# A recurrent layer whose odd chunks swap partition halves between the two heads of a pair

## The chip, the cores and the metric

The kernel runs on one core of a Trainium2 chip. Five engines work side by side on that core: TensorE (PE in the profile, with its weight loads as PEld), VectorE (DVE), ScalarE (ACT), GpSimd (POOL) and SyncE (SP), which here issues most DMAs. The metric is the device time of one execution in microseconds (us). The kernel before took 1336.81 us, the median of three runs between 1336.61 and 1337.48 us. A difference below about 0.2% can't be told from no change.

TensorE's array has 128 rows and 128 columns. The rows that a matmul uses are the partitions of its two operands, the columns are the partitions of its result in PSUM. A product with 64 rows and 64 columns therefore uses one quarter of the array, called a quadrant here and written (row half to column half): (0 to 0), (0 to 64), (64 to 0), (64 to 64).

## The reference

The reference is a two-layer encoder trunk on 512 frames of width 1024. Layer 0 mixes time by an RWKV-7 recurrence with 12 heads of 64 and attends to 256 memory tokens, layer 1 mixes by attention over chunks, and each is followed by a convolutional gated feed-forward part. The change concerns only the recurrence of layer 0, whose state is updated frame by frame:

```python
def step(state, inp):
    r_t, w_t, k_t, v_t, a_t, b_t = inp
    sa = jnp.einsum('bhvk,bhk->bhv', state, a_t)
    state = (state * w_t[:, :, None, :] + sa[..., None] * b_t[:, :, None, :]
             + v_t[..., None] * k_t[:, :, None, :])
    return state, jnp.einsum('bhvk,bhk->bhv', state, r_t)
```

Around it, projections give r, k, v, a and the decay w, and the result y is normalised per head, gets a bonus term and is multiplied by a gate.

## The kernel before

The 512 frames are cut into 8 chunks of 64, and the 12 heads into 6 pairs. A pair fills the 128 partitions: head 0 lies on partitions 0 to 63 (`HS[0]`), head 1 on 64 to 127 (`HS[1]`). The recurrence is computed in its chunked form. Within a chunk everything becomes products of 64 by 64 blocks, the coupling of the frames inside a chunk is a triangular system whose inverse is built from blocks of 16 and 32, and only the state is handed from chunk to chunk.

Three Python generators issue the work of a pair. `prepare` does the three dense projections (24 weight tiles, three matmuls of 128x512 each), the keys and decays `KB`, `AR`, `E`, and the inversion of the 16-blocks on DVE with four small DMA round trips. `front` multiplies `KB` by `AR` into the masked table `ML` (line 879, evicted by DVE at 882), turns `AR` and `v` into rows in `VT` (`rows_av`, lines 903 and 905, evicted by ACT at 907), turns `KB` into rows (893, evicted at 896), and joins the inverse blocks to 32 in `Tt`. `back` does the rest:

- transposes the inverse blocks on DVE (984), and multiplies a 32-block of `ML` by them (989), evicted by ACT into `X5` (993);
- multiplies `ML` by the value rows (997), evicted into slot 2 of `VT` (998);
- completes the inverse to 64 (1003, evicted at 1007);
- applies the inverse to slots of `VT` (1013), evicted into `W` (1014) and back into `VT` (1016);
- multiplies `W` by `ML` (1024), evicted by DVE into `MQ` (1025, 1026);
- forms the chunk's contribution to the state `G` (1032, 1033) and the output inside the chunk (1041), runs the chain over chunks (1046, 1047, 1051), normalises and gates.

Each fp32 matmul of the program appears as two instructions in the trace, so the 16 products (8 chunks, 2 heads) of a step count as 32. The results of 997 and 989 for all eight chunks lie in one PSUM bank. Steps 1013 and 1024 are done in two halves of four chunks, one bank and one `yield` each. In all these steps the two heads of one chunk alternate, and both head's products use the same two quadrants for every chunk: (0 to 0) and (64 to 64) in 1013 and 1024, (64 to 0) and (0 to 64) in 997. Only `rows_av` visits all four: head h goes (h to h) for `AR` and (h to 1-h) for `v`.

The order of the work is set by `weave`. It holds, for each generator, the sum of the costs that it has yielded, divided by an expected total, and lets the one go on that is furthest behind; a second number in a `yield` keeps a generator away for that many planner nanoseconds. Weave number st runs `back` of pair st-1, `front` of pair st and `prepare` of pair st+1 together, so the dense matmuls of `prepare` fill the time in which the small products wait for evictions. A last weave runs `back` of pair 4, `front` and `back` of pair 5, the memory attention, and part of the output projection. The framework's scheduler may still move an instruction past another that it holds not ready. Each engine then works strictly through its own list.

Small products go to a PSUM pool "S" of four banks, shared by `front`, `back`, `prepare` and the memory attention. `psy` and `psc` have a pool of two, dense projections another two. A bank is given out again when its eviction is done.

Of the kernel before, what the change touches and what calls it, by code (L numbers as in the profile page):

```python
# [18 lines left out]
P = 128  # L19
# [93 lines left out]
def trunk_kernel(ctx, tc, A, out):  # L113
# [40 lines left out]
    def ups():  # L154
        return ps_s((P, 8, 64))
# [547 lines left out]
    U = [(c, h, HS[h], HS[1 - h]) for c in range(NCH) for h in range(2)]  # L703
    MC = 16 * 80

    d2s = [dp.tile([2, 8, 2, 4, NCH, 32], F32, name="d2" + "ab"[n_], tag="d2" + "ab"[n_]) for n_ in range(2)]

    def prepare(i, T):
# [160 lines left out]
    def front(i, T, nxt=None):  # L869
# [4 lines left out]
        for c4 in range(2):  # L874
            ps = [ps_s((P, 4, 128)) for _ in range(2)]
            for c in range(4):
                cc = c4 * 4 + c
                for h in range(2):
                    PE.matmul(ps[h][:, c], KB[HS[h], cc, 1 - h:3 - h].rearrange("p s t -> p (s t)"),
                              AR[HS[h], cc].rearrange("p s t -> p (s t)"), start=True, stop=True)  # L880
            for h in range(2):
                V.tensor_tensor(ML[:, h, c4 * 4:c4 * 4 + 4, 0:128], ps[h][:],
                                C("m1").unsqueeze(1).to_broadcast([P, 4, 128]), op=ALU.mult)
            yield 1000
# [4 lines left out]
        def rows_kb():  # L889
            ps = [ups(), ups()]  # L890
            for c in range(8):
                for h in range(2):
                    PE.transpose(ps[h][:, c], KB[HS[h], c, 1 - h:3 - h].rearrange("p s t -> p (s t)"),
                                 cst[HS[h], I64:I64 + 64])
            for h in range(2):
                SC.copy(ML[:, h, :, 128:192], ps[h][:])


        def rows_av():
            ps = [ups(), ups()]  # L900
            for c in range(8):
                for h in range(2):
                    PE.matmul(ps[h][HS[h], c], AR[HS[h], c, 0], cst[HS[h], I64:I64 + 64], start=True, stop=True)
                for h in range(2):
                    PE.matmul(ps[h][HS[1 - h], c], v[HS[h], c], C("blkc", h * 64, 64)[HS[h]], start=True, stop=True)
            for h in range(2):
                SC.copy(VT[:, h], ps[h][:])

        rows_av()
        yield 1000  # L910
# [68 lines left out]
    def back(i, T, dst, tiles=own_tiles, go=None):  # L979
        Rq, dE, bon, ML, VT, Tt = (T[n] for n in ("Rq", "dE", "bon", "ML", "VT", "Tt"))  # L980
        W, MQ, X5, Tl, g2h, g2l, bank = tiles()

        for lo in (slice(0, 32), slice(64, 96)):
            V.transpose(Tl[lo], Tt[lo, :, 0:32])

        ps = ups()
        for c, h, ap, vp in U:
            lo, hi_ = slice(h * 64, h * 64 + 32), slice(h * 64 + 32, h * 64 + 64)
            PE.matmul(ps[hi_, c, 0:32], ML[lo, h, c, 32:64], Tl[lo, c], start=True, stop=True,
                      tile_position=(h * 64, h * 64 + 32))  # L990
        for h in range(2):
            hi_ = slice(h * 64 + 32, h * 64 + 64)
            SC.copy(X5[hi_], ps[hi_, :, 0:32])
        yield 650
        ps = ups()
        for c, h, ap, vp in U:
            PE.matmul(ps[ap, c], ML[vp, h, c, 0:64], VT[vp, h, c], start=True, stop=True)
        SC.copy(VT[:, 2], ps[:])
        yield MC
        ps = ups()  # L1000
        for c, h, ap, vp in U:
            lo, hi_ = slice(h * 64, h * 64 + 32), slice(h * 64 + 32, h * 64 + 64)
# [3 lines left out]
            lo = slice(h * 64, h * 64 + 32)  # L1006
            SC.copy(Tt[lo, :, 32:64], ps[lo, :, 0:32])
        yield 650, 400
        for c4 in (slice(0, 4), slice(4, 8)):
            ps = ps_s((P, 4, 2, 64))  # L1010
            for c in range(c4.start, c4.stop):
                for h in range(2):
                    PE.matmul(ps[HS[h], c % 4], Tt[HS[h], c], VT[HS[h], h:3:2 - h, c], start=True, stop=True)
            SC.copy(W[:, c4], ps[:, :, 0])
            for h in range(2):
                SC.copy(VT[HS[h], h, c4], ps[HS[h], :, 1])
            yield 1100
        G, St = VT[:, 2], W
        yield 0, 300
        for c4 in (slice(0, 4), slice(4, 8)):  # L1020
            ps = ps_s((P, 4, 128))
            for c in range(c4.start, c4.stop):
                for h in range(2):
                    PE.matmul(ps[HS[h], c % 4], W[HS[h], c], ML[HS[h], h, c, 64:192], start=True, stop=True)
            V.tensor_tensor(MQ[:, c4, 64:128], ps[:, :, 64:128], C("i64").unsqueeze(1).to_broadcast([P, 4, 64]), op=ALU.add)
            V.tensor_tensor(MQ[:, c4, 0:64], ps[:, :, 0:64], Rq[:, c4], op=ALU.add)
            yield 1100
        g2 = tmp(F32, (P, P))
        nc.sync.dma_start(g2, A["g2"][i])
        psg = ups()  # L1030
        for c, h, ap, vp in U:
            PE.matmul(psg[ap, c], ML[:, h, c, 128:192], VT[:, h, c], start=True, stop=True)
# [5 lines left out]
        psy = bank((P, 8, 64))  # L1038
        for c in range(8):
            for h in range(2):  # L1040
                PE.matmul(psy[HS[h], c], VT[:, h, c], ML[:, h, c, 64:128], start=c == 0, stop=False)
        yield 1700
        for c in range(8):
            if 0 < c < 7:
# [27 lines left out]
        dst(i, yc, pg)  # L1072
        yield 1080

    BACK_COST = 2 * 650 + 2 * MC + 4 * 1100 + 1700 + 6 * 150 + 7 * 150 + 700 + 1080

    mixd = dp.tile([4, P, S], F32, name="mixd", tag="mixd")

# [455 lines left out]
```

## Time and profile before

| Quantity | Value |
| --- | --- |
| Median of three runs | 1336.81 us (1336.61 to 1337.48) |
| Span of the profiled execution, first to last instruction | 1335.7 us |
| What lies around the span, median less span | 1.1 us |
| PE busy over the span | 1308.9 us (98%) |
| DVE and ACT busy | 926.4 us and 683.5 us |
| Stretch with the six weaves | about 88 to 345 us |
| Mean granted TensorE clock | 0.995 |

In the profile a line number is that of the kernel before. A group or timeline row names the engine, the line, the operation, the tile written and the tiles read, the part of the array (rows*columns), the moving operand's shape, and the count. Timeline rows begin with the start and the length. A matmul's length contains its passage through the array, so the pace of a series is read from the start of the series to the start of what follows, divided by the count. In square brackets stands idle time before an instruction, and what ended it.

### The profile page before, as it was taken

The page shows a single profiled execution, that of the slowest core. Times are in us where ns is not written, and L with a number is a line of the kernel's source. Part 1 is how long each engine was busy: PE and PEld are TensorE (multiplying, and loading weights), DVE is VectorE, ACT ScalarE, POOL GpSimd, SP SyncE. Part 2 cuts the span into 40 slices and gives each one's busy share as a digit, 9 for nine tenths or more (in the row PEclk, how much of TensorE's full clock was granted, in tenths as well). Part 3 has the DMA queues.
Part 4 walks back from the last instruction along what each step waited for, and adds up shares of the span by engine and source line. Part 5 has one row for each costly group of instructions (what it writes and reads, how often), then busy time and mean ns, then how long its engine had stood idle before and what let it go on. Part 6 is the DMA issues. An engine that isn't in the chain of part 4 may idle for free. (4 is left out here: it accounts for less than half of the span.)

```text
span 1335.7 us, 24426 instructions
## 1 busy us (share of the span) xinstructions
PE 1308.9 (98%) x9838; PEld 1099.3 (82%) x9838; DVE 926.4 (69%) x1822; ACT 683.5 (51%) x1166; POOL 20.1 (2%) x45
## 2 busy tenths in 40 slices
PE   9999999999999999999999999999999999999996
PEld 7787777777788899998888877786888999988885
DVE  7966766766669898887343675657689988893224
ACT  6666656665445445464232576657454444562221
POOL 0000000000000000000000000000000000000000
PEclk9999999999999999999999999999999999999998
DMA  5365344351232434223333323241324423223322
GB/s 197 110 187 109 88 96 96 86 115 55 96 105 84 142 95 127 71 64 98 94 107 104 120 87 96 88 130 51 111 87 134 124 67 111 80 76 103 100 87 78
DMA packets 65730, 135.42 MB, mean 101 GB/s; under 512 B 19792, under 2 KB 25296, under 8 KB 65616
## 3 DMA queue, kind: packets, MB, share of 16 engines
q1 hardware_dynamic: 63168, 124.94, 30.7%
q0 software_dynamic: 2448, 8.91, 3.8%
q8 instruction: 77, 1.26, 0.4%
q14 instruction: 37, 0.30, 0.1%
HBM read 127.53 MB, written 6.29 MB: 100 GB/s over the span
## 5 line engine op out<-in xcount | busy, mean ns | idle before, releaser
L176 DVE TENSOR_TENSOR wlo<-wraw,whi 128x1024 fp32r<-128x1024 f32 (+1 forms) x139 | 165.4, 1190 | 143.0 <-PE psd L208 131.3
L170 ACT CAST whi<-wraw 128x1024 fp32r<-128x1024 f32 (+1 forms) x156 | 159.9, 1026 | 167.3 <-DMA wraw<-in_ffn_out_dram 51.7
L204 PE MATMUL psd<-r1h,whi 128*128 128x512 f32 (+1 forms) x383 | 152.3, 399 | 0.1
L205 PE MATMUL psd<-r1l,whi 128*128 128x512 f32 x320 | 126.0, 394 | 0.0
L170 ACT CAST whi<-raw 128x1024 fp32r<-128x1024 f32 x88 | 82.9, 943 | 76.0 <-PE psf L420 41.8
L176 DVE TENSOR_TENSOR wlo<-raw,whi 128x1024 fp32r<-128x1024 f32 x88 | 95.6, 1086 | 15.2 <-ACT whi L170 15.2
L208 PE MATMUL psd<-r1h,wlo 128*128 128x512 f32 (+1 forms) x383 | 104.2, 397 | 0.0
L204 PEld LDWEIGHTS psd<-r1h,whi 128*128 128x128 f32 x383 | 72.0, 188 | 16.7 <-issue 2.7
L208 PEld LDWEIGHTS psd<-r1h,wlo 128*128 128x128 f32 x383 | 68.6, 188 | 14.7 <-issue 1.4
L420 PE MATMUL psf<-r2h,whi 128*128 128x256 f32 x308 | 77.3, 283 | 0.5 <-ACT tmp L442 0.5
L420 PE MATMUL psf<-r2l,whi 128*128 128x256 f32 x308 | 77.2, 283 | 0.0
L204 PE MATMUL psd<-r2h,whi 128*128 128x512 f32 (+1 forms) x184 | 71.1, 390 | 0.1
L205 PE MATMUL psd<-r2l,whi 128*128 128x512 f32 (+1 forms) x184 | 69.9, 383 | 0.0
L238 ACT ACTIVATE tmp<-xT 128x512 f32<-128x512 f32 x27 | 17.0, 631 | 103.0 <-DVE xT L497 88.3
L205 PEld LDWEIGHTS psd<-r1l,whi 128*128 128x128 f32 x320 | 60.2, 188 | 10.9 <-issue 0.2
L420 PEld LDWEIGHTS psf<-r2h,whi 128*128 128x128 f32 x308 | 59.1, 192 | 0.9 <-ACT tmp L442 0.7
L420 PEld LDWEIGHTS psf<-r2l,whi 128*128 128x128 f32 x308 | 59.1, 192 | 0.2
L422 PE MATMUL psf<-r2h,wlo 128*128 128x256 f32 x308 | 49.5, 283 | 0.0
L208 PE MATMUL psd<-r2h,wlo 128*128 128x512 f32 (+1 forms) x184 | 47.1, 386 | 0.0
L393 ACT ACTIVATE tmp<-tmp 128x512 f32<-128x512 f32 x44 | 27.7, 630 | 33.6 <-DVE tmp L392 33.1
L420 PE MATMUL psf<-r1h,whi 128*128 128x256 f32 x176 | 44.2, 284 | 0.3 <-ACT tmp L442 0.3
L204 PE MATMUL psd<-hl,whi 128*128 128x512 f32 (+1 forms) x119 | 44.4, 377 | 0.0
(468 smaller groups left out, 3326.7 us busy)
## 6 DMA issues: line engine op xcount, KB each, us to landing
wraw<-in_ffn_in_dram SPq DMA_DIRECT2D x44, 512.0 KB, 3.6
raw<-in_ffn_in_dram SPq DMA_DIRECT2D x88, 256.0 KB, 4.1
wraw<-in_ffn_out_dram SPq DMA_DIRECT2D x32, 448.0 KB, 3.3
wraw<-in_wA_dram SPq DMA_DIRECT2D x20, 512.0 KB, 4.1
wraw<-in_w_out_dram SPq DMA_DIRECT2D x16, 512.0 KB, 3.6
wraw<-in_ffn_out_dram SPq DMA_DIRECT2D x16, 512.0 KB, 3.5
wlo<-in_wA_dram POOLq DMA_DIRECT2D x15, 512.0 KB, 6.6
wraw<-in_wB_dram SPq DMA_DIRECT2D x8, 512.0 KB, 3.6
```

The lines of the kernel that those rows point to most:

```text
L170: SC.copy(hi[:, :n], raw)
L176: V.tensor_tensor(lo[:, :n], raw, hi[:, :n], op=ALU.subtract)
L204: PE.matmul(ps, wh[:, j * P:(j + 1) * P], ah, start=start and n == 0, stop=False)
L205: dense_at[0] = PE.matmul(ps, wh[:, j * P:(j + 1) * P], al, start=False, stop=False)
L208: dense_at[0] = PE.matmul(ps, wl[:, j * P:(j + 1) * P], act(k)[0], start=False, stop=stop and n == len(ks) - 1)
L238: SC.activation(sq[:], src, AF.Square)
L393: SC.activation(c[:], c[:], AF.Gelu)
L420: PE.matmul(ps, wh[:, o + k * P:o + k * P + P], x[k][n], start=k == n == 0, stop=False)
L422: PE.matmul(ps, wl[:, o + k * P:o + k * P + P], x[k][0], start=False, stop=k == 3)
```

## The change

For an odd chunk the slots of the two heads are exchanged. `slot(c, h)` is `h` for an even chunk and `1 - h` for an odd one. `front` builds `ML` and the rows of `KB` with the halves exchanged for odd chunks, and `rows_av` writes even and odd chunks separately. In `back` the steps 989, 997, 1013 and 1024 take chunks in the order of `four()`: an even chunk's two heads, then the next odd chunk's two heads, and the four products lie in four different quadrants. The even chunks' results go to one bank, the odd chunks' to another. Steps 1013 and 1024 are no longer cut in halves of four chunks; the planner's costs and waits are changed with them. The transposes (984) and most evictions become one instruction for each parity, on every second chunk.

```diff
+    def slot(c, h):
+        return h ^ (c & 1)
+    def four():
+        for c2 in range(4):
+            for par in range(2):
+                for h in range(2):
+                    c = c2 * 2 + par
+                    yield c, c2, par, h, slot(c, h)
+    def par_of(t, par):
+        return t.rearrange("p (a e) t -> p a e t", e=2)[:, :, par]
...
-                PE.matmul(ps[h][:, c], KB[HS[h], cc, 1 - h:3 - h].rearrange("p s t -> p (s t)"),
+                u = slot(cc, h)
+                PE.matmul(ps[h][:, c], KB[HS[h], cc, 1 - u:3 - u].rearrange("p s t -> p (s t)"),
...
         def rows_av():
-            ps = [ups(), ups()]
-            for c in range(8):
+            ev = [ps_s((P, 4, 128)) for _ in range(2)]
+            for c2 in range(4):
                 for h in range(2):
-                    PE.matmul(ps[h][HS[h], c], AR[HS[h], c, 0], cst[HS[h], I64:I64 + 64], start=True, stop=True)
+                    PE.matmul(ev[h][HS[h], c2, 0:64], AR[HS[h], c2 * 2, 0], cst[HS[h], I64:I64 + 64], start=True, stop=True)
                 for h in range(2):
-                    PE.matmul(ps[h][HS[1 - h], c], v[HS[h], c], C("blkc", h * 64, 64)[HS[h]], start=True, stop=True)
+                    PE.matmul(ev[h][HS[1 - h], c2, 0:64], v[HS[h], c2 * 2], C("blkc", h * 64, 64)[HS[h]],
+                              start=True, stop=True)
             for h in range(2):
-                SC.copy(VT[:, h], ps[h][:])
+                SC.copy(par_of(VT[:, h], 0), ev[h][:, :, 0:64])
+            od = ps_s((P, 2, 4, 64))
+            for c2 in range(4):
+                for h in range(2):
+                    PE.matmul(od[HS[h], h, c2], AR[HS[h], c2 * 2 + 1, 0], cst[HS[h], I64:I64 + 64], ...)
+                for h in range(2):
+                    PE.matmul(od[HS[h], 1 - h, c2], v[HS[h], c2 * 2 + 1], C("blkc", h * 64, 64)[HS[h]], ...)
+            for n in range(2):
+                SC.copy(par_of(VT[:, n], 1), od[:, n])
...
-        for lo in (slice(0, 32), slice(64, 96)):
-            V.transpose(Tl[lo], Tt[lo, :, 0:32])
+        for par in range(2):
+            for h in range(2):
+                u = h ^ par
+                V.transpose(par_of(Tl[u * 64:u * 64 + 32], par), par_of(Tt[h * 64:h * 64 + 32, :, 0:32], par))
+        ps = [ps_s((P, 4, 128)) for _ in range(2)]
+        for c, c2, par, h, u in four():
+            lo, hi_ = slice(u * 64, u * 64 + 32), slice(h * 64 + 32, h * 64 + 64)
+            PE.matmul(ps[par][hi_, c2, 0:32], ML[lo, h, c, 32:64], Tl[lo, c], start=True, stop=True,
+                      tile_position=(u * 64, h * 64 + 32))
+        for par in range(2):
+            for h in range(2):
+                hi_ = slice(h * 64 + 32, h * 64 + 64)
+                SC.copy(par_of(X5[hi_], par), ps[par][hi_, :, 0:32])
         yield 650
-        ps = ups()
-        for c, h, ap, vp in U:
-            PE.matmul(ps[ap, c], ML[vp, h, c, 0:64], VT[vp, h, c], start=True, stop=True)
-        SC.copy(VT[:, 2], ps[:])
-        yield MC
+        ps = [ps_s((P, 4, 128)) for _ in range(2)]
+        for c, c2, par, h, u in four():
+            PE.matmul(ps[par][HS[h], c2, 0:64], ML[HS[1 - u], h, c, 0:64], VT[HS[1 - u], u, c], start=True, stop=True)
+        for par in range(2):
+            SC.copy(par_of(VT[:, 2], par), ps[par][:, :, 0:64])
+        yield MC / 2
...
-        for c4 in (slice(0, 4), slice(4, 8)):
-            ps = ps_s((P, 4, 2, 64))
-            for c in range(c4.start, c4.stop):
-                for h in range(2):
-                    PE.matmul(ps[HS[h], c % 4], Tt[HS[h], c], VT[HS[h], h:3:2 - h, c], start=True, stop=True)
-            SC.copy(W[:, c4], ps[:, :, 0])
-            for h in range(2):
-                SC.copy(VT[HS[h], h, c4], ps[HS[h], :, 1])
-            yield 1100
+        ps = [ps_s((P, 4, 2, 64)) for _ in range(2)]
+        for c, c2, par, h, u in four():
+            PE.matmul(ps[par][HS[u], c2], Tt[HS[h], c], VT[HS[h], h:3:2 - h, c], start=True, stop=True)
+        for par in range(2):
+            SC.copy(par_of(W, par), ps[par][:, :, 0])
+            for u in range(2):
+                SC.copy(par_of(VT[HS[u], u], par), ps[par][HS[u], :, 1])
+        yield 1100
         G, St = VT[:, 2], W
-        yield 0, 300
-        for c4 in (slice(0, 4), slice(4, 8)):
-            ps = ps_s((P, 4, 128))
-            for c in range(c4.start, c4.stop):
-                for h in range(2):
-                    PE.matmul(ps[HS[h], c % 4], W[HS[h], c], ML[HS[h], h, c, 64:192], start=True, stop=True)
-            ...
-            yield 1100
+        yield 0, 900
+        ps = [ps_s((P, 4, 128)) for _ in range(2)]
+        for c, c2, par, h, u in four():
+            PE.matmul(ps[par][HS[h], c2], W[HS[u], c], ML[HS[u], h, c, 64:192], start=True, stop=True)
+        ...
+        yield 1100
...
-    BACK_COST = 2 * 650 + 2 * MC + 4 * 1100 + 1700 + 6 * 150 + 7 * 150 + 700 + 1080
+    BACK_COST = 2 * 650 + 1.5 * MC + 2 * 1100 + 1700 + 6 * 150 + 7 * 150 + 700 + 1080
```

Steps 1032 and 1041 only read the exchanged slots (`VT[:, u, c]`), and step 1003 is as before.

More of the change, by code (lines that the diff above doesn't have):

```diff
@@ L1031, in back @@
         for c, h, ap, vp in U:
-            PE.matmul(psg[ap, c], ML[:, h, c, 128:192], VT[:, h, c], start=True, stop=True)
+            u = slot(c, h)
+            PE.matmul(psg[ap, c], ML[:, h, c, 128:192], VT[:, u, c], start=True, stop=True)
         V.tensor_tensor(G, psg[:], dE[:].unsqueeze(2).to_broadcast([P, NCH, 64]), op=ALU.mult)
@@ L1040, in back @@
             for h in range(2):
-                PE.matmul(psy[HS[h], c], VT[:, h, c], ML[:, h, c, 64:128], start=c == 0, stop=False)
+                u = slot(c, h)
+                PE.matmul(psy[HS[h], c], VT[:, u, c], ML[:, h, c, 64:128], start=c == 0, stop=False)
         yield 1700
```

22 lines of the change are left out of this document (11 added, 11 removed).

## The prediction

> **What bounds the kernel now.** I read the page first, then busy time in the stretch with the six weaves and in one weave alone (start and end, length, then busy time and count for PE, weight loads, DVE, ACT, POOL, the granted clock, the DMA share and GB/s), then what PE waited for in that stretch (with total us, times, longest).
>
> ```profile
> span 1335.7 us, 24426 instructions
> PE 1308.9 (98%) x9838; PEld 1099.3 (82%) x9838; DVE 926.4 (69%) x1822; ACT 683.5 (51%) x1166; POOL 20.1 (2%) x45
> ...
> 88.00:345.00 257.00, 250.73 (x3869) 192.07 (x3867) 173.18 (x530) 161.14 (x340) 13.84 (x16) 1.00 0.42 91
> 156.80:199.70 42.90, 41.97 (x657) 32.28 (x655) 30.52 (x95) 27.28 (x54) 2.60 (x3) 1.00 0.45 96
> ...
> PE pss L1013 <- ACT Tt L1007: 1.6, 2, 1.0
> PE pss L997 <- DVE ML L882: 1.3, 3, 0.4
> ```
>
> PE is busy for 250.7 of 257 us of the recurrence, at the full granted clock, and its longest kinds of wait add up to a few us over six pairs. DVE (173) and ACT (161) have a third of the stretch free. A product that leaves PE sooner therefore lets the next one start sooner, unless that one must now wait. Whether PE is only occupied or also at its pace is read from starts in the timeline of PE, in the second weave (start, length, engine, line):
>
> ```profile
> 156.86 0.69 PE L989 MATMUL pss<-Tl,ML 32*32 32x32 f32 x32
> 157.48 1.16 PE L879 MATMUL pss<-AR,KB 64*128 64x128 f32 x16
> ...
> 160.67 1.15 PE L997 MATMUL pss<-VT,ML 64*64 64x64 f32 x32 [0.45 <-DVE ML L882]
> 161.75 0.69 PE L1003 MATMUL pss<-Tt,X 32*32 32x32 f32 x32
> 162.37 1.16 PE L879 MATMUL pss<-AR,KB 64*128 64x128 f32 x16
> 163.47 1.09 PE L1013 MATMUL pss<-VT,Tt 64*64 64x128 f32 x16
> 164.49 0.96 PE L208 MATMUL psd<-r1h,wlo 128*128 128x512 f32 x3
> 165.38 1.09 PE L1013 MATMUL pss<-VT,Tt 64*64 64x128 f32 x16
> 166.40 1.20 PE L208 MATMUL psd<-r1h,wlo 128*128 128x512 f32 x4
> 167.43 0.39 PE L204 MATMUL psd<-r1h,whi 128*128 128x512 f32 x1
> 167.66 0.39 PE L205 MATMUL psd<-r1l,whi 128*128 128x512 f32 x1
> ...
> 168.44 0.28 PE L903 MATMUL pss<-cst,AR 64*64 64x64 f32 x2
> 168.45 0.27 PE L905 MATMUL pss<-cst,v 64*64 64x64 f32 x2
> ...
> 169.37 0.23 PE L905 MATMUL pss<-cst,v 64*64 64x64 f32 x2
> 169.53 0.51 PE L204 MATMUL psd<-r1h,whi 128*128 128x512 f32 x1
> ...
> 170.19 1.09 PE L1024 MATMUL pss<-ML,W 64*64 64x128 f32 x16
> 171.21 0.50 PE L204 MATMUL psd<-r1h,whi 128*128 128x512 f32 x1
> ```
>
> The row pair that decides is this. Step 997 puts 32 instructions on two quadrants in 161.75 - 160.67 = 1.08 us, 34 ns each. `rows_av` (903 and 905) puts 32 + 32 of the same shape on all four quadrants in 169.53 - 168.44 = 1.09 us, 17 ns each. A quadrant thus takes about 68 ns for one of them in both cases, and four run beside each other where two did. Steps 1013 and 1024 (128 moving columns, two quadrants) take 164.49 - 163.47 = 1.02 us for 16, 64 ns each. Four quadrants were never tried on that shape here.
>
> On the same row half a rule speaks against the change. The Trainium skill, TensorE: Matmul & The Clock Gate, Part 3 (Packing small matmuls — row/col tiling), says that a weight load overlaps a matmul in flight only when its row group differs. Two quadrants of one row half would then take turns and bring nothing; `rows_av`, which alternates on both row halves at twice the rate, does not bear that out for this shape. What that would make of the time is rival 4.
>
> **The change, part by part (per pair, then times six).**
>
> 1. Step 997 goes from two quadrants to four: 1.08 us becomes 32 x 17 ns = 0.55, a gain of 0.53.
> 2. Step 989 (157.48 - 156.86 = 0.62 us for 32) goes from two 32x32 tiles to four. Halved like 997: gain 0.31. Bounds: 0 and 0.31.
> 3. Steps 1013 and 1024 take 2 x 1.02 us each. At half the pace each is 1.02, a gain of 1.02 + 1.02. Bounds: 0, and 2.04 in all; I take the whole, as the nearest row, the 64-column one, doubled fully.
> 4. `rows_av` loses. For odd chunks both `AR` and `v` of head h now go (h to h): only two quadrants. Even chunks: 32 instructions at 17 ns = 0.55. Odd chunks: 32 at 34 = 1.08. Sum 1.63 against 1.09, a loss of 0.54.
> 5. The merged halves save two visits to the dense stream. A dense matmul follows the last at 0.23 us (167.43 to 167.66); the visit of three between the halves of 1013 took 165.38 - 164.49 = 0.89 instead of 0.69. Bounds for two such visits: 0 and 0.4; I take 0.2, half, since a switch remains wherever other work falls between.
> 6. Steps 879, 893, 1003, 1032, 1041, the scan and the DMAs keep their count and shape; SP's and POOL's queues get nothing new. The exchanged slices of `KB` cost nothing, since they are the same rows and columns.
>
> Gain on PE: 0.53 + 0.31 + 2.04 - 0.54 + 0.2 = 2.54 us per pair, 15.2 us for six.
>
> Against it stand the evictions, from the groups of the same stretch (busy, mean ns, then idle before) and rows of the ACT and DVE timelines:
>
> ```profile
> L907 ACT COPY VT<-pss 128x512 f32<-128x512 f32 x12 | 6.4, 587 | 3.0 <-PE pss L905 2.9
> L1014 ACT COPY W<-pss 128x256 f32<-128x256 f32 x10 | 3.7, 372 | 3.0 <-PE pss L1013 2.9
> L1016 ACT COPY VT<-pss 64x256 f32<-64x256 f32 x24 | 8.8, 367 | 0.2
> L993 ACT COPY X<-pss 32x256 f32<-32x256 f32 x10 | 3.6, 364 | 10.0 <-PE pss L989 10.0
> L998 ACT COPY VT<-pss 128x512 f32<-128x512 f32 x6 | 3.5, 586 | 0.7 <-PE pss L997 0.6
> L984 DVE STREAM_TRANSPOSE Tl<-Tt 32x256 f32<-32x256 f32 x10 | 4.3, 431 | 1.7 <-ACT Tt L959 1.5
> ...
> 161.36 0.68 DVE L882 TENSOR_TENSOR ML<-pss,cst 128x512 f32<-128x512 f32 x1
> ...
> 167.63 1.06 ACT L173 ACTIVATE wlo<-wraw 128x1024 fp32r<-128x1024 f32 x1
> 168.71 0.72 ACT L744 ACTIVATE krv<-tmp,om 128x512 f32<-128x512 f32 x1
> ...
> 171.00 1.07 ACT L907 COPY VT<-pss 128x512 f32<-128x512 f32 x2
> ```
>
> 7. More and shorter copies on ACT. From 586 ns for 512 columns and 372 for 256, a copy shrinks by 0.84 ns a column, so 32x128 is estimated at 364 - 107 = 257 ns. `rows_av`: 4 x 372 - 2 x 587 = +0.31; `X5`: 4 x 257 - 2 x 364 = +0.30; 998: 2 x 372 - 586 = +0.16. Sum +0.77 us per pair. On DVE the four half transposes, bounded by the same time in all and by twice it, add 0 to 0.86. Both engines have a third of the stretch free, so I count nothing for them, except that the copies of 998 stand ahead of those of 1007, for which PE waited in two of six pairs: 2 x 0.16 = 0.3 in all. Without the free third it would be 4.6 us for ACT.
> 8. Banks at the start of a weave. Steps 989 and 997 ask for two of the four banks instead of one, beside the two of 879, at a place where the rows show small products back to back (161.75, 162.37, 163.47) and no dense matmul between. PE already waits 0.45 us there for the eviction 882. Waiting for the second 882 as well, which ends at 161.36 + 0.68 = 162.04, costs 162.04 - 160.67 = 1.37. Bounds 0 and 1.37; I take 0.5, one more wait like the one seen, in the five full weaves: 2.5.
> 9. Banks around `rows_av`. It takes three banks, 1024 two at once, that is five of four. ACT came to the copies 907 at 171.00, 1.5 us after PE had finished at 169.53, and 1024 began at 170.19. Waiting for the first copy, cut to 0.37, would end at 171.37, 1.2 us later. But dense matmuls are ready there and the scheduler may put them first. Bounds 0 and 1.2; I take 0.3, five times: 1.5.
> 10. The wait from 1013 to 1024. The second half's copies ran beside other work; now `W` is whole only after W, VT, VT, W: 2 x 372 + 2 x 367 = 1.48 us after 1013. In full weaves 3.8 us of other work lay between (166.40 to 170.19), and the new planner wait keeps 0.9: I count 0 there. In the last weave nothing lies between for pair 5:
>
> ```profile
> 318.86 1.96 PE L1013 MATMUL pss<-VT,Tt 64*64 64x128 f32 x32
> 320.65 2.04 PE L1024 MATMUL pss<-ML,AR 64*64 64x128 f32 x32
> ```
>
> There 1024 would wait the 1.48 (and 0.1 for the hand-over, 1.6), so most of its gain is lost. For pair 4 I take 0.3. Sum 1.9; bounds 0 and 6 x 1.48 = 8.9.
>
> Sum: -15.2 + 0.3 + 2.5 + 1.5 + 1.9 = -9.0 us. The profiled execution: 1335.7 - 9.0 = 1326.7. The runs' median lies 1.1 above that span, so I forecast 1327.8 us, 0.7% faster.
>
> **The rivals.**
>
> 1. The whole gain: all four stall terms are nothing because the scheduler puts dense work wherever a bank or `W` is late. 1336.8 - 15.2 = 1321.6. For it: so little waiting today. Against it: the weave starts and pair 5 have no dense work to put there.
> 2. No change that can be measured: the stalls of 8 and 9 at their upper ends (6.9 + 6.0) and 10 as taken eat the gain: -15.2 + 0.3 + 12.9 + 1.9 = -0.1, 1336.7 us. For it: the bank waits of 997 are there today. Against it: a list of instructions is planned with these banks in mind.
> 3. Slower, by one mechanism: 1024 held by ACT. ACT works in order, and if the weight cast of 173 (1.06 us) and the 744 activation (0.72) stand ahead of the copies, the second half of `W` is ready 1.06 + 0.72 + 1.48 = 3.26 us after 1013, with no dense matmul issued between. It decides from 2.54 us per pair on. Price 0.72 per pair, 4.3 us in all: 1341.1. For it: both instructions stood right behind the copies at 167.63. Against it: the 0.9 us planner wait and the 3.8 us of work seen in that gap. The Trainium skill, TensorEngine Tiling (Array Packing), Performance Considerations, PSUM Bottleneck, warns that packing the array speeds TensorE but not the emptying of PSUM; that ACT and DVE have a third of the stretch free speaks against it here.
> 4. The quadrants of one row half take turns. Then 1 to 3 gain nothing, 4 loses its 0.54 as the pace of `rows_av` is a row of the trace, and 5 and 7 to 10 stay: 6 x (0.54 - 0.2) + 6.2 = +8.2 at most, without the stalls +2.0. 1338.8 to 1345.
>
> **How the numbers follow.** The forecast gets 0.52 with its own range of 1324 to 1333 (stall terms between a third and half as much again), rival 1 0.17, rival 2 0.10, rival 3 0.15, rival 4 0.06. A difference under 0.2%, 2.7 us, can't be told from none. Faster: 0.52 + 0.17 = 0.69; same 0.10; slower 0.21. The range runs from 1320, which holds rival 1, to 1340, which leaves out about half of rivals 3 and 4 and little else, so some 0.85 is meant to lie inside.
>
> **What would show it.** In the profile after, 32 instructions of 997 should take about 0.55 us from start to start, 1013 and 1024 about 1.0 each in one piece, 989 about 0.3, and `rows_av` about 1.6 with its odd half at 34 ns. PE waits should grow at 997, 989 or 879 for DVE's 882, and at 1024 for ACT's W copies in pair 5. The stretch of the weaves should shrink by about 9 us and the rest of the span stay. The prediction is wrong if the pace of 1013 stays at 64 ns, or if PE's idle time in the weaves grows by more than 15 us, or if the new order moves the scan over chunks to where no dense work is left.

## The result and the profile after

The changed kernel takes 1349.5 us (median of four runs, 1348.74 to 1350.96) against 1337.14 (1336.61 to 1338.06) for the kernel before beside it: ratio 1.0092, 95% interval 1.008 to 1.0104. It is slower by 0.9%, where 0.7% faster was forecast. Its profiled execution took 1350.19 us, with a span of 1348.4: 12.7 us more than before.

The pages differ little (the first two lines of the page after). The stretch of the six weaves, in the same columns as before, and parts of it in windows of 4 us, differ much:

```profile
span 1348.4 us, 24498 instructions
...
PE 1311.2 (97%) x9838; PEld 1099.4 (82%) x9838; DVE 927.0 (69%) x1834; ACT 688.8 (51%) x1196; POOL 20.5 (2%) x45
```

```profile
88.00:345.00 257.00, 240.67 (x3764) 183.23 (x3765) 163.88 (x506) 160.11 (x354) 13.80 (x16) 0.97 0.41 92
...
128.00:132.00 4.00, 0.19 (x14) 0.05 (x4) 3.12 (x12) 1.44 (x2) 0.06 (x1) 0.85 0.83 133
132.00:136.00 4.00, 3.95 (x50) 3.21 (x52) 0.56 (x2) 1.93 (x5) 0.00 (x0) 0.50 0.69 175
136.00:140.00 4.00, 4.00 (x37) 3.11 (x36) 0.69 (x1) 0.32 (x2) 0.00 (x0) 0.79 0.04 7
...
328.00:332.00 4.00, 3.52 (x103) 2.75 (x105) 3.56 (x12) 3.44 (x12) 0.00 (x0) 1.00 0.01 4
332.00:336.00 4.00, 4.00 (x51) 2.85 (x43) 0.93 (x2) 1.91 (x7) 0.00 (x0) 0.53 0.40 131
336.00:340.00 4.00, 4.00 (x42) 2.77 (x38) 1.48 (x4) 3.08 (x11) 0.00 (x0) 0.50 0.01 4
```

In the same stretch PE got through 3764 of its instructions instead of 3869, and it was busy 240.7 us instead of 250.7. Twice in it, the granted clock fell to a half. The lengths of these spells, from the trace's record of the clock, are 6.83 and 10.24 us, two and three times 3.41.

The weaves tell where the 12.7 us arose. A period here runs from the start of the X5 step (989 before, 1022 after) to the next one; the last runs to the start of the memory attention's last product (line 313). Further line numbers after the change: 997 is 1031, 1013 is 1046 with its copies 1048 and 1050, 1024 is 1056 with DVE's 1058 and 1060, `rows_av` is 923 and 925 for even chunks (copied by 928), 932 and 935 for odd ones (938); 879 is 898, 882 is 901.

| Period, us | before | after | `oldnum_wait` (below) |
| --- | --- | --- | --- |
| weave 1 | 44.8 | 54.0 | 45.4 |
| weave 2 | 42.8 | 44.6 | 41.2 |
| weave 3 | 42.8 | 44.6 | 41.2 |
| weaves 4 and 5 together | 105.6 | 104.4 | 99.9 |

That is +9.1, +1.8, +1.8 and -1.2; the first period begins 0.9 us later, and the rest of the span is equal within 0.3 us (987.6 before, 987.9 after).

**Steady weaves.** The timeline of PE in weave 2 after the change (start, length, engine, line) and that of ACT at the same place:

```profile
173.49 1.10 PE L1046 MATMUL pss<-VT,Tt 64*64 64x128 f32 x32
174.52 0.50 PE L205 MATMUL psd<-r1l,whi 128*128 128x512 f32 x1
174.86 0.40 PE L204 MATMUL psd<-r1h,whi 128*128 128x512 f32 x1
175.10 0.40 PE L205 MATMUL psd<-r1l,whi 128*128 128x512 f32 x1
176.21 0.65 PE L1056 MATMUL pss<-ML,W 64*64 64x128 f32 x6 [0.72 <-ACT W L1048]
177.25 0.77 PE L1056 MATMUL pss<-ML,W 64*64 64x128 f32 x19 [0.39 <-ACT W L1048]
```

```profile
175.05 0.72 ACT L762 ACTIVATE krv<-tmp,om 128x512 f32<-128x512 f32 x1
175.79 0.37 ACT L1048 COPY W<-pss 128x256 f32<-128x256 f32 x1
176.06 0.74 ACT L1050 COPY VT<-pss 64x256 f32<-64x256 f32 x2
176.82 0.37 ACT L1048 COPY W<-pss 128x256 f32<-128x256 f32 x1
```

The merged step 1046 has the forecast pace: 32 instructions from 173.49 to 174.52. But only three dense matmuls stand behind it, and then PE is at 1056 and stands still for 0.72 and 0.39 us. ACT reaches the first copy of `W` only at 175.79, behind the activation of 762, and ends the last at 177.19, 2.67 us after 1046.

**Weave 1** has a hole. Timelines of PE, then DVE:

```profile
126.62 1.10 PE L1056 MATMUL pss<-ML,W 64*64 64x128 f32 x32
...
132.05 0.48 PE L932 MATMUL pss<-cst,AR 64*64 64x64 f32 x4 [3.86 <-DVE MQ L1060]
```

```profile
121.83 0.36 DVE L830 TENSOR_TENSOR Xu<-Lr,cst 128x120 f32<-128x120 f32 x1 [2.17 <-DMA Lr<-d]
...
130.49 0.75 DVE L763 SCALAR_TENSOR_TENSOR krv<-tmp,vec,krv 128x511 f32<-128x511 f32 x1 [0.71 <-ACT krv L762]
131.15 0.42 DVE L1058 TENSOR_TENSOR MQ<-pss,cst 128x256 f32<-128x256 f32 x1
131.49 0.41 DVE L1060 TENSOR_TENSOR MQ<-pss,Rq 128x256 f32<-128x256 f32 x1
131.82 0.42 DVE L1058 TENSOR_TENSOR MQ<-pss,cst 128x256 f32<-128x256 f32 x1
```

1056 now runs ahead of the odd half of `rows_av`, which needs one of the banks that 1056 filled. DVE begins to empty them only at 131.15 and has the first one free at 131.90, because its inversion for the next pair, which began late behind a DMA, stands ahead, and then 763, which waits for ACT. `rows_av` stands next in PE's list, so PE does nothing for 3.9 us, and the first spell of half clock begins within this hole, at 130.8.

### The profile page after: what moved, and what is told of

The parts are those of the page before. It is cut to its first block, busy times and chain, and to the rows that moved or that the text cites. A ratio compares the mean times of both kernels' runs of the same rounds, so it can differ in the third digit from the quotient of the medians.

```text
span 1348.4 us, 24498 instructions
## 1 busy us (share of the span) xinstructions
PE 1311.2 (97%) x9838; PEld 1099.4 (82%) x9838; DVE 927.0 (69%) x1834; ACT 688.8 (51%) x1196; POOL 20.5 (2%) x45
## 5 line engine op out<-in xcount | busy, mean ns | idle before, releaser
L238 ACT ACTIVATE tmp<-xT 128x512 f32<-128x512 f32 x27 | 17.1, 632 | 104.8 <-DVE xT L497 89.0
L204 PE MATMUL psd<-hl,whi 128*128 128x512 f32 (+1 forms) x119 | 44.4, 377 | 0.0
L205 PE MATMUL psd<-sl,whi 128*128 128x512 f32 (+1 forms) x119 | 44.4, 377 | 0.0
L205 PE MATMUL psd<-hl,whi 128*128 128x512 f32 (+1 forms) x119 | 44.3, 376 | 0.0
```

The costliest lines, as they stand in the source:

```text
L204: PE.matmul(ps, wh[:, j * P:(j + 1) * P], ah, start=start and n == 0, stop=False)
L205: dense_at[0] = PE.matmul(ps, wh[:, j * P:(j + 1) * P], al, start=False, stop=False)
L238: SC.activation(sq[:], src, AF.Square)
```

## The experiments

Medians, ratios to the kernel before with the 95% interval, and, from each profiled execution, the span, the length of half-clock spells in the weaves (from the record of the clock), and the period of weave 2:

| Run | Median, us | Ratio | Span | Half clock, us | Weave 2, us |
| --- | --- | --- | --- | --- | --- |
| `oldnum` | 1334.6 | 0.9977 (0.9967 to 0.9986) | 1332.6 | 3.4 | 41.2 |
| `newnum` | 1340.42 | 1.0022 (1.0011 to 1.0033) | 1339.5 | 6.8 | 43.3 |
| `twoq` | 1346.45 | 1.0069 (1.0054 to 1.0084) | 1346.1 | 6.8 | 44.5 |
| `filler` | 1344.7 | 1.0052 (1.0035 to 1.0069) | 1345.4 | 6.8 | 44.6 |
| `rowsfirst` | 1349.0 | 1.0091 (1.0075 to 1.0108) | 1345.5 | 20.5 | 44.3 |
| `wfirst` | 1348.54 | 1.0085 (1.007 to 1.01) | 1344.9 | 10.2 | 44.6 |
| `twoq_old` | 1336.26 | 0.9992 (0.9983 to 1.0002) | 1333.4 | 0 | 42.2 |
| `oldnum_fill` | 1336.43 | 0.9995 (0.9986 to 1.0004) | 1333.6 | 3.4 | 41.3 |
| `steps2200` | 1352.53 | 1.0096 (1.0066 to 1.0127) | 1344.2 | 6.8 | 44.8 |
| `mc1280` | 1351.59 | 1.0102 (1.0081 to 1.0122) | 1349.6 | 27.3 | 44.3 |
| `oldnum_wait` | 1331.49 | 0.9953 (0.9936 to 0.9969) | 1330.9 | 0 | 41.2 |
| `oldnum_L` | 1344.18 | 1.0053 (1.0038 to 1.0068) | 1342.2 | 20.5 | 42.1 |
| `before_wait` | 1336.7 | 0.9992 (0.9984 to 1.0001) | 1334.9 | 0 | 42.5 |
| `after_w300` | 1349.94 | 1.0087 (1.0074 to 1.01) | 1347.3 | 10.2 | 44.9 |

The kernel before has no half clock in its weaves, the changed one 17.1 us. The profiled execution need not be a typical one: that of `filler` was its slowest (1347.21 us), and that of `steps2200` (1345.97) lies far below its median.

**The quadrants and the planner's numbers, each alone.** `oldnum` is the changed kernel with the numbers of before, `newnum` the kernel before with the changed numbers:

```diff
# oldnum, against the changed kernel
-        yield MC / 2
+        yield MC
-        yield 1100            (after 1046 and after 1056)
+        yield 2200
-        yield 0, 900
+        yield 0, 300
-    BACK_COST = 2 * 650 + 1.5 * MC + 2 * 1100 + ...
+    BACK_COST = 2 * 650 + 2 * MC + 4 * 1100 + ...
# newnum, against the kernel before: MC -> MC / 2, 1100 -> 550 for each half, 300 -> 900, the new BACK_COST
```

> The changed kernel with the planner's numbers of before in the back generator (1280 for the value product, 2200 for each of the two merged steps, wait 300, the old expected total). Theory A (the order that the new numbers make is at fault: in the first full weave rows_av comes behind step 1056, its third bank waits 3.86 us for the DVE eviction of 1056, and the low activity halves the TensorE clock for 6.8 us): rows_av stands ahead of 1056 again, hole and first half-clock spell go, 3.9 + 3.4 = 7.3 us less than the changed kernel, about 1342 us. Rival B (the loss is many small bank and copy waits in every weave, whatever the order): within 2 us of the changed kernel's 1349.5.

> The kernel before with the planner's numbers of the change (half for the value product, 550 for each half of 1013 and 1024, wait 900, the new expected total); products, banks and evictions as before. Theory A (the order alone can do damage): slower than before by 3 us or more, about 1340 to 1345, with PE waits or a half-clock spell in the weaves. Rival B (the order is harmless, the three banks of rows_av and the merged steps do it): within 2 us of 1337.

With the old numbers the change gains: 1334.6 us, 0.9977, twice as far below the changed kernel as theory A had it. With the new ones it loses, and the new numbers cost the kernel before 0.2% by themselves. So the quadrants are worth -0.2% under the old numbers and +0.7% (1.0092 against 1.0022) under the new: the two parts don't add up, they interact.

**Is the pace real?** `twoq` is meant to take away the use of four quadrants and to keep all else: it loops over all even chunks first, then all odd ones. `twoq_old` does this to `oldnum`.

```diff
-        for c2 in range(4):
-            for par in range(2):
+        for par in range(2):
+            for c2 in range(4):
                 for h in range(2):
```

> The changed kernel with the order of products inside the four steps changed: all products of even chunks, then all of odd chunks, so that only two quadrants work at a time; banks, evictions and planner numbers stay. Theory A (the four quadrants do gain on TensorE and the loss is elsewhere): the two-quadrant pace returns, 0.53 + 0.3 + 2.04 us per pair, up to 17 us more than 1349.5 where nothing hides it, at least 8. Rival B (what the quadrants gain is swallowed by waits for copies and banks): within 3 us of 1349.5.

> The kernel with the planner's numbers of before, and in the four steps all even chunks first and then all odd ones, so that two quadrants work at a time. Theory A (TensorE is the bound in the weaves, the four quadrants pay what their pace says): up to 0.23 + 0.5 + 2.0 us more per pair than oldnum's 1334.6, about 16 us for six, at least 10: 1345 to 1351. Rival B (stalls would have hidden most of it): 1335 to 1340.

`twoq` is 3 us faster than the changed kernel, although its packing is worse, and it has 10.2 us less of half clock. It can't tell, since the two effects are mixed. `twoq_old` can: in weave 2 steps 1046 and 1056 take 0.49 us longer each and 1022 0.15, and weaves 2, 3 and 4 are each 1.0 longer. There the pace on PE reaches the period almost whole. The run is only 1.7 us longer, since weave 1 is 1.5 us shorter (46.2 against 47.6): `oldnum`'s spell of half clock isn't there. Its time, 1336.26 us, lies where rival B had it and not at 1345 or more, but stalls are not the reason; the step itself lost half of what was expected. Its timeline shows why:

```profile
165.09 1.59 PE L1046 MATMUL pss<-VT,Tt 64*64 64x128 f32 x32
...
171.58 1.59 PE L1056 MATMUL pss<-ML,W 64*64 64x128 f32 x32
```

Two quadrants in a row should cost the 2.04 us of before; from first start to last end it is 1.59, and by starts 1.52. PE has begun odd products in free quadrants ahead of even ones still queued: in 1046 two chains of starts, 109 ns apart each, overlap. The even chunks' chain runs from 165.09 to 165.90, the odd chunks' begins at 165.59, though in the program's list every odd product stands behind all even ones. So `twoq_old` takes away only half of the packing.

**Is it the order of 1056 and `rows_av`?** In the changed kernel 1056 runs ahead of `rows_av`, in the kernel before 1024 runs behind it. `rowsfirst` restores that order alone, by the costs of `front`: its first two yields of 1000 become 790 each, and the 800 behind the rows of `KB` becomes 1220. `wfirst` tests the wait for `W`, by making both copies of `W` ahead of those of `VT`.

> The changed kernel with two planner numbers of front altered, sum kept: the first yield of 1000 (both halves of 898) becomes 790, the 800 behind the rows of KB becomes 1220. By shares of the expected totals rows_av then comes up at 1580 of 5400 x 1.069, 27.4%, ahead of step 1056 at 3040 of 10850 x 1.003, 27.9%, where in the changed kernel it came up at 34.6%, behind 1056. Everything else is as in the changed kernel. Theory A (the order of rows_av and 1056 is the cause of the loss): waits of rows_av for the eviction of 1056 and of 1056 for the W copies go, 1334 to 1339 us. Rival B (the other shares matter, for instance how much dense work is left for the chain over chunks): over 1343.

> The changed kernel with both copies into W ahead of the four copies back into VT. The second W copy is then ready about 0.7 us earlier. Theory A (1056 comes too early behind 1046 and waits for that copy, 2.8 us in all by the list of PE's waits): that wait goes from the list, 2 to 4 us less than 1349.5, and the large waits of rows_av stay. Rival B (that wait only stands in for another): within 1.5 us of 1349.5.

`rowsfirst` closes the hole of weave 1 (54.0 to 47.9 us), and still takes 1349.0: weaves 2 and 3 keep 44.3 each, and weaves 4 and 5 take 3.6 us longer than in the changed kernel and hold all of its 20.5 us of half clock. The order explains the hole, not the loss. `wfirst` can't be told from the changed kernel. PE's waits for `W` fall in all from 2.8 to 1.7 us, and its waits for DVE's `MQ` right behind, at 932, rise from 5.0 to 5.4; weave 2 keeps its 44.6 us. With so little dense work at that place, one wait seems to have been exchanged for the next.

**Which number?** `steps2200` restores only the cost of the merged steps, `mc1280` only the `yield` after 1031; `BACK_COST` follows.

> The changed kernel with only the yields of the two merged steps put back to 2200 each (what four halves of 1100 came to), and 2200 more in the expected total; the 640 for the value product and the wait of 900 stay. rows_av comes ahead of 1056 again. Theory C (the small costs of the two merged steps bring the rest of back too early in every weave, so that evictions are awaited and dense matmuls are used up): near oldnum, 1334 to 1338. Rival D (the 640 for the value product or the wait of 900 does it): over 1343.

> The changed kernel with only the yield of the value product put back to 1280, and 640 more in the expected total; the merged steps keep 1100 and the wait 900. rows_av comes ahead of 1056 here too. Theory C: little is mended beside the first weave, 1342 to 1349. Rival D (the value product's number matters): under 1340.

Neither helps by its median. The executions of `steps2200` are spread from 1344.44 to 1355.38 us, but its fastest is still 12 us over the slowest of `oldnum_wait` below (1332.65). Then the wait, which stands at 900 in the changed kernel and at 300 before:

```diff
# oldnum_wait, against oldnum; before_wait, against the kernel before; after_w300 the other way round
-        yield 0, 300
+        yield 0, 900
```

> The kernel with the planner's numbers of before, but the wait of 900 behind step 1046 instead of 300. Theory C: no matter, 1333 to 1337. Rival D (the longer wait does harm by moving the later chain): over 1340.

> The kernel before with the wait ahead of step 1024 raised from 300 to 900 planner nanoseconds, and nothing else. It asks how much of the gain of oldnum_wait (1331.5 us) is the four quadrants and how much the longer wait. If the quadrants bring their saving by themselves (the saved time of steps 1013 and 1024 is kept wherever the planner's proportions stand), this kernel stays near 1337, between 1335 and 1339. If the longer wait alone makes the difference between oldnum (1334.6) and oldnum_wait, it comes to about 1334, 3 us under before.

> The changed kernel with the wait ahead of step 1056 put back from 900 to 300, its other planner numbers kept as changed. If the costs and not the wait lose the time, it stays near after's 1349.5, between 1346 and 1353, with a spell of half clock in the weaves again. If the longer wait is what stops the back part and lets it be late, it falls to 1340 or below.

The wait doesn't lose the time (`after_w300` is at 1349.94), and alone it does not gain any that can be told (`before_wait`). With both old costs it brings the best version: 1331.49 us, better than both kernels. Against `before_wait`, which has the same wait and the same costs in all but works with two quadrants, that is 0.4% (0.9953 against 0.9992), some 5 us for the quadrants where the forecast had 9.0. It differs from `oldnum` in weave 1 (45.4 against 47.6), where the spell is gone, and in the last (55.4 against 58.2). At a wait of 900 the table of costs is thus complete: both new 1349.5, only the steps restored 1352.53, only the `yield` restored 1351.59, both restored 1331.49. The order on PE in weave 2, read from the starts, says why:

```
before       879b, 1013 half, 3 dense, 1013 half, 8 dense, rows_av, 2 dense, 1024 half, 4 dense, 1024 half, 8 dense
oldnum_wait  898b, 1046, 11 dense, rows_av, 6 dense, 1056, 8 dense
after        898b, 1046,  3 dense, 1056 with rows_av,      2 dense
mc1280       898b, 1046,  3 dense, rows_av, 1056,          4 dense
steps2200    4 dense, 1046, 898b, rows_av, 1056,           9 dense
newnum       879b, 1013, 3 dense, 1024 with rows_av,       2 dense
```

(898b is the second half of 898.) Wherever a merged step is charged 1100, the planner leaves three dense matmuls, 0.7 us of work, between it and what uses its banks or its `W`; the copies of `W` end 2.67 us behind 1046 in the changed kernel, and still 2.03 behind it in `oldnum_wait`, where 762 no longer stands ahead of them. Where it is charged 2200 but the step before it only `MC / 2`, 1046 comes ahead of 898b, and 898b, `rows_av` and 1056 then ask in one piece for banks, some of which 1046's copies still hold (923 waits 5.9 us in all for 1050). Only with both is there dense work at each such place. The timeline of PE in `oldnum_wait`, then that of ACT:

```profile
166.19 1.10 PE L1046 MATMUL pss<-VT,Tt 64*64 64x128 f32 x32
167.23 1.88 PE L208 MATMUL psd<-r1h,wlo 128*128 128x512 f32 x7
...
169.94 0.27 PE L923 MATMUL pss<-cst,AR 64*64 64x64 f32 x2
...
171.28 0.28 PE L935 MATMUL pss<-cst,v 64*64 64x64 f32 x4
171.49 0.50 PE L204 MATMUL psd<-r1h,whi 128*128 128x512 f32 x1
...
173.07 1.10 PE L1056 MATMUL pss<-ML,W 64*64 64x128 f32 x32
174.11 0.50 PE L204 MATMUL psd<-r1h,whi 128*128 128x512 f32 x1
```

```profile
167.85 0.37 ACT L1048 COPY W<-pss 128x256 f32<-128x256 f32 x1
168.12 0.75 ACT L1050 COPY VT<-pss 64x256 f32<-64x256 f32 x2
168.89 0.37 ACT L1048 COPY W<-pss 128x256 f32<-128x256 f32 x1
```

What PE waited for (total us, times, longest) over the weaves, in the changed kernel and then in `steps2200`, `mc1280` and `oldnum_wait`; the first two lines of each:

```profile
PE pss L932 <- DVE MQ L1060: 5.0, 4, 3.9
PE pss L1056 <- ACT W L1048: 2.8, 6, 0.7
```

```profile
PE pss L923 <- ACT VT L1050: 5.9, 6, 1.4
PE pss L985 <- ACT Y L974: 2.3, 6, 1.0
```

```profile
PE pss L1056 <- ACT VT L928: 5.2, 4, 3.1
PE pss L985 <- ACT Y L974: 2.1, 3, 1.4
```

```profile
PE pss L1056 <- ACT VT L928: 1.1, 1, 1.1
PE pss L985 <- ACT Y L974: 1.1, 5, 0.3
```

**The half clock.** `filler` adds two useless dense products to the changed kernel, one before `rows_av` of pair 1, one before 1022 of pair 5, where spells begin. `oldnum_fill` does the first in `oldnum`.

```diff
+            if i == 1:
+                PE.matmul(ev[0][:].rearrange("p a b -> p (a b)"), C("ident"), cst[:, 0:512], start=True, stop=True)
# in filler also a like product into ps[0], ahead of 1022, if i == NPAIR - 1
```

> The changed kernel with two useless 128x128 by 128x512 products added, one ahead of rows_av of pair 1 and one ahead of step 1022 of pair 5, each into a bank that is overwritten after. They add about 0.85 us of TensorE work each. Theory A (the clock is halved because too little of the array works in a stretch of 3.4 us): one or both half-clock spells (6.8 and 10.2 us) go, so that the kernel gets faster by 3 to 7 us although it does more, 1343 to 1346. Rival B (the clock has nothing to do with the array's work, or the spells cost nothing since other engines are late anyway): 1 to 2 us slower than 1349.5.

> The kernel with the planner's numbers of before and one useless 128x128 by 128x512 product (0.85 us) ahead of rows_av of pair 1, into a bank that is overwritten after. Theory A (the half-clock spell of 3.4 us that oldnum still has in its first full weave comes from too little work in the array, and the product falls into a wait for ACT that is there anyway): the spell goes, 1 to 2 us less than oldnum's 1334.6. Rival B (the spell has another cause): 0 to 1 us more than oldnum.

With more work, `filler` is 4.8 us faster than the changed kernel, and its spells fall from 17.1 to 6.8 us. Its stretch of the weaves, in the same columns as above, shows hardly more busy PE, but a granted clock of 0.99 instead of 0.97:

```profile
88.00:345.00 257.00, 242.08 (x3797) 182.72 (x3797) 164.26 (x508) 161.29 (x356) 13.81 (x16) 0.99 0.42 93
```

A spell of T us can cost up to T/2: 10.2 us less should bring up to 5.1. In `oldnum_fill` the one spell stayed, and the kernel became 1.8 us slower: there my filler was at the wrong place or too little, and the theory that one product suffices falls. What the table shows without any theory: every kernel under 1338 us has 0 or 3.4 us of half clock, and every one above 1340 has 6.8 to 27.3. Which of the two is the cause, the table doesn't say.

What a spell costs can be estimated from executions of one and the same kernel. Those of `steps2200` took 1344.44, 1345.97, 1352.53, 1353.29 and 1355.38 us at mean granted clocks of 0.993, 0.993, 0.986, 0.983 and 0.982. From the first to the last the clock falls by 0.011, which is some 30 us more at half clock, and the time grows by 10.9: about 0.37 us for each us of half clock. `mc1280`, from 1347.44 us at 0.990 to 1353.93 at 0.984, gives 0.4. This is an estimate, since the spells themselves were recorded for the profiled executions alone.

**The banks at the start of a weave.** `oldnum_L` takes the odd banks of 1022 and 1031 from the pool of `psy` and `psc`, except in the last pair, and else is `oldnum`.

```diff
-        ps = [ps_s((P, 4, 128)) for _ in range(2)]
+        ps = [ps_s((P, 4, 128)), (ps_l if bank is ps_l else ps_s)((P, 4, 128))]
# in both steps
```

> The kernel with the planner's numbers of before; the odd chunks' bank of steps 1022 and 1031 comes from the pool of two banks that psy and psc use, except in the last pair. Theory (the two banks of each of these steps keep 898 and the second half of 1031 waiting at the start of a weave, 0.9 and 0.6 us by the starts): both waits go, up to 1.5 us in each of four weaves, 1329 to 1333. Rival (898 and 1031 wait for something else): 1333.5 to 1336.

The wait for which it was made goes (898 from 3.10 to 2.18 us in weave 2, from start to start), yet others come, 1056 waits, and half clock of 20.5 us:

```profile
PE pss L1056 <- ACT VT L928: 3.1, 3, 2.0
PE psl L1077 <- issue: 2.9, 1, 2.9
```

A bank that is freed at one place sends PE sooner to the next place where nothing is ready. How much of its 9.6 us over `oldnum` is the clock and how much the waits stays open.

## Why the prediction was wrong

Slots of PE in weave 2, each from a start to the next start, summed by step, in us:

| Step | before | `oldnum_wait` | after | Forecast change |
| --- | --- | --- | --- | --- |
| 989 / 1022 | 0.62 | 0.38 | 0.38 | -0.31 |
| 997 / 1031 | 1.08 | 1.22 | 1.22 | -0.53 |
| 1013 / 1046 | 2.04 | 1.03 | 1.03 | -1.02 |
| 1024 / 1056 | 2.04 | 1.03 | 1.72 | -1.02 |
| `rows_av` | 1.09 | 1.55 | 2.25 | +0.54 (+0.3) |
| 879 / 898 | 2.18 | 3.10 | 2.87 | +0.5 |
| dense, 72 in each | 20.32 | 19.43 | 21.72 | -0.2 |
| period | 42.84 | 41.21 | 44.60 | -1.7 |

The sum of the forecast's terms for a full weave was -2.54 + 0.05 + 0.5 + 0.3 = -1.7 us; with the planner's old costs (`oldnum_wait`) it is -1.63. That the two agree so well is in part luck: step 1 brought 0.67 us less than forecast for 1031, step 8 cost 0.42 more, while step 5, which brought 0.69 more, and `rows_av`, which cost 0.38 less with its wait, make up for it. For the whole kernel the forecast missed by 21.7 us. 18.0 of them lie between the changed kernel and `oldnum_wait`, which differ in the planner's costs alone; 3.7 stay with the old costs too. The mechanism of the pace was right, and what the edit of the costs does to the order was not seen. By its steps:

- **Steps 1 to 4, the pace.** 1046 and 1056 at half the time, 1022 a little above it, `rows_av` a little under its forecast loss: right. Step 1 failed for 1031 in weaves 2 to 4: in weave 2 it comes in two groups of 0.61 us each, with other work let in between, and gains nothing (timeline of PE in the changed kernel). Within a group the starts come in pairs, 58 ns apart, so only two quadrants are in use at a time: in PE's list the products of one parity stand ahead of a dense matmul, and the other's, which need a bank that ACT empties, stand behind it. Where the list keeps 1031 whole, for pair 4, the same kernel takes 0.62 us for it (298.55 to 299.17), near the 0.55 forecast; so the pace was right and the list broke the step up.

```profile
170.11 0.68 PE L1031 MATMUL pss<-VT,ML 64*64 64x64 f32 x16
170.72 0.51 PE L204 MATMUL psd<-r1h,whi 128*128 128x512 f32 x1
171.16 0.68 PE L1031 MATMUL pss<-VT,ML 64*64 64x64 f32 x16
171.77 0.69 PE L1038 MATMUL pss<-Tt,X 32*32 32x32 f32 x32
```

- **Step 5** was too small: in `oldnum_wait` there are fewer visits, and the same 72 dense matmuls take 0.89 us less, of which 0.42 is a wait ahead of 997 that has gone.
- **Step 7** was right: a copy of 32x128 takes 257 ns, as estimated from the two longer ones (columns: busy, mean ns, idle before). As far as the runs show, neither engine became the bound by it.

```profile
L1027 ACT COPY X<-pss 32x128 f32<-32x128 f32 x20 | 5.1, 257 | 4.0 <-PE pss L1022 3.8
L1048 ACT COPY W<-pss 128x256 f32<-128x256 f32 x10 | 3.7, 372 | 2.7 <-PE pss L1046 2.5
```

- **Step 8**, 0.5 a weave, measured 0.92 for 898 alone in `oldnum_wait`; inside its bounds. Steps 8 and 9 were counted for five full weaves, but only weaves 1 to 4 run all three generators.
- **Step 10 is the step that failed.** It counted 0 in full weaves, on the ground that 3.8 us of other work lay between 1013 and 1024 and that "the new planner wait keeps 0.9". The 3.8 us were the doing of the planner's costs, and the change lowers those: `MC` to `MC / 2`, a merged step from 2200 to 1100. I read these lines as bookkeeping and gave them no term. They took the dense work from between the steps: between 1046 and 1056 stand 17 dense matmuls and `rows_av` in `oldnum_wait`, three dense matmuls in the changed kernel. The planner wait of 900 kept nothing (`after_w300`, without it, takes 1349.94). Weave 2 has no half clock in either kernel, so the 3.4 us that the changed one takes longer there are the order's alone. The dense term shows the rest of the price: the same 72 cost 2.3 us more than in `oldnum_wait`, 0.7 of it up to 1067 (the wait ahead of 1056 seen above), 0.6 from 1067 to 985, where the dense matmuls now come in eleven visits instead of seven, at about 0.2 for a switch, and 1.0 at the weave's end, where none are left to cover two waits (690 for ACT, 699 for DVE).
- **Step 9**, 0.3 with an upper bound of 1.2, broke its bound in weave 1: 3.9 us. It bounded the wait by ACT's copies; the bank was held by DVE's `MQ`, since the order of 1056 and `rows_av` had turned, which the bound supposed fixed.
- **The half clock has no term** in the sum. The kernel before ran its weaves at a full granted clock, and I took that as given. 17.1 us at half clock can cost up to 8.5 us; by the 0.37 to 0.4 estimated above it is 6 to 7 of the 12.7 us. That the new costs bring the spells is shown (none in `oldnum_wait`); which property of their order does it is not.

Of the rivals, the fourth is false (1046 halved). The third named the right mechanism (ACT's 744, now 762, ahead of the copies, and hardly a dense matmul between, three in the trace), but priced it at 4.3 us in all, and saw "the 0.9 us planner wait" as speaking against it. Of the signs named for a failure, PE's idle time grew by 10 us in the stretch, not by 15, since half clock counts as busy.

## What to carry to other kernels

Where a planner orders the work, its costs are part of the kernel: a step that becomes twice as fast may need its old cost, because the cost decides how much other work stands behind it until its eviction is done. Cost such a line as an edit of the order, by listing what will then stand next to what, and test an optimisation with the planner's numbers held fixed before they are retuned. Look at the granted clock of every candidate: the same packing had 17.1 us of half clock in its weaves under one order and none under another.

## What the hardware showed

- The granted clock fell to a half without a long pause of PE. From 328 to 332 us PE was busy for 3.52 of 4 us, but with products of 32x32 and 64x64. Weighted with their share of the array's cells (an fp32 column at 0.85 ns, from the 109 ns at which one quadrant repeats 128 columns), the 3.4 us before that spell come to about 0.2 of the array; the lowest such stretch in the weaves of before, where the clock stayed whole, to about 0.25. The other traces give no threshold: `twoq` keeps the whole clock behind a stretch of about 0.24 (325.0 to 328.4 us), `newnum` loses it behind 0.26 (334.4 to 337.8, PE busy throughout), and `oldnum` behind 0.35 or more (128.1 to 131.5, PE busy for half of it). The Trainium skill, TensorE: Matmul & The Clock Gate, Part 1 (The HAM clock gate), says that a monitor of PE's activity sets the clock to a half or to full, in free-running windows of 3413 ns. The spells here are multiples of 3.41 us, which agrees. That the use of the array counts beside PE's being busy is what some of these rows suggest; of the two runs that test it, `filler` speaks for it and `oldnum_fill` doesn't, so it is not shown.
- A half-clock spell slows small products to little more than half their pace: from its start to the next row's, step 1067 took 1.91 us there and 1.08 in `oldnum_wait`. A dense matmul had a length of 0.63 to 0.79 us in the spell, 0.40 to 0.50 in the steady weave above. Timeline of the changed kernel, then of `oldnum_wait`:

```profile
134.54 0.63 PE L205 MATMUL psd<-r1l,whi 128*128 128x512 f32 x1
135.10 1.98 PE L1067 MATMUL pss<-VT,ML 128*64 128x64 f32 x32
137.00 0.79 PE L204 MATMUL psd<-r1h,whi 128*128 128x512 f32 x1
```

```profile
176.14 1.15 PE L1067 MATMUL pss<-VT,ML 128*64 128x64 f32 x32
177.23 0.71 PE L913 MATMUL pss<-cst,KB 64*128 64x64 f32 x16
```

- Four quadrants run side by side also with 128 moving columns: the 32 instructions of 1046 in 1.03 us, 32 ns each, two of the quadrants in each row half. And PE does not work strictly through its list, as was said of every engine at the start: the two chains of starts in `twoq_old`, and its 1.52 us against 2.04.
